# Pooling stage of a two-layer decoder trunk: the pool scale as one split row spread by TensorE, small loads moved, mixing reordered

## The chip, the cores and the metric

One core of a Trainium2 chip runs the whole program. The metric is the device time of one execution in microseconds. A core has five engines with queues of their own that run side by side and meet at semaphores: TensorE (PE; its weight loads are PEld), VectorE (DVE), ScalarE (ACT), GpSimd (POOL) and SyncE (SP). SP, ACT and POOL issue the DMAs. Each engine works its instructions strictly in the order in which the kernel issues them.

## The reference

A trunk of two layers over 512 tokens of width 1024, all float32. Layer 0 mixes tokens by causal pooling in four channel groups, layer 1 by differential attention; after each mixer and each FFN stands a LayerNorm over ALPHA times the input plus the branch. The change touches the pooling mixer alone:

```python
def _multiscale_pool(x, w, scale):
    xg = x.astype(jnp.float32).reshape(B, S, N_GROUPS, GROUP_W)
    cs = jnp.pad(jnp.cumsum(xg, axis=1), ((0, 0), (1, 0), (0, 0), (0, 0)))
    for g, win in enumerate(POOL_WINDOWS):          # 2, 4, 8, 16
        hi = cs[:, 1:, g]
        lo = jnp.pad(cs[:, :S + 1 - win, g], ((0, 0), (win - 1, 0), (0, 0)))
        cnt = jnp.minimum(t + 1, win).astype(jnp.float32)[None, :, None]
        pooled.append((hi - lo) / cnt)
    pooled = jnp.stack(pooled, axis=2)
    mixed = jnp.einsum('bsgc,gcd->bsgd', pooled - xg, w.astype(jnp.float32))
    return (mixed.reshape(B, S, D) * scale.astype(jnp.float32)).astype(x.dtype)

def reference(...):
    for i in range(DEPTH):
        ...
        x = _layernorm(ALPHA * x + h, ln_mix_g[i], ln_mix_b[i])
        x = _layernorm(ALPHA * x + _swiglu(x, w_gate[i], w_up[i], w_down[i]), ln_ffn_g[i], ln_ffn_b[i])
    return x
```

## The kernel before

Matrix products run in fp32r: each operand is split into a rounded high part and the rest, its low part, and three matmuls (high x high, high x low, low x high) make one product (`mm3`). The high part is a cast by ACT, the low part a subtraction by DVE (`split`; one time by POOL). After the pooling stage come the first FFN (`ffn(0, ...)`), the attention and the second FFN; their code is the same in both kernels. The first FFN's first matmuls read `xt`, the normed and transposed tokens 0 to 255, and the weight tiles w2 and w3; then w4 and w5 with the transposes of token blocks 2 and 3 between them.

The pooling stage works on four token blocks of 128 (`res[:, s]`, loaded by `load_x(s)`). Its steps, in the kernel's order:

- Loads. SP issues x block 0, x block 1, the first half of the pool scale (512 channels, broadcast over 128 partitions by the load itself), weight tile raw 0 (`fetch`), x block 2, the scale's second half, raw 1, x block 3, raw 2. ACT issues `d0`, the 16 x 16 corner with the counts of the first tokens. POOL issues four small loads: the rows of the LayerNorm gains and biases (`lrows`, two loads), the bias table (`tb`) and the one-hot lines (`oh_`).
- Constants. POOL makes `after`, a distance table, and `ident`. DVE makes `band` (L291) out of it: for each group a 128 x 144 matrix with 1/w where a token falls into the window, 128 columns for the block itself and 16 for the tail that reaches into the next block. `edge` is the same for block 0, with `d0` copied into its corner by ACT (L298). DVE subtracts the identity (L297), since the mixer takes pooled minus x.
- Warm-up. Seven matmuls on a zero tile (L303), in two records each.
- `shares(half, s, source, a, b, ...)` (L329): eight float32 matmuls, 16 records, that spread token block s over the accumulators `made[half, g]` of its half of the tokens: columns a to b of band or edge are the moving operand. The order on TensorE is: block 0 (144 columns), block 1 (128 columns), block 1's tail into the second half (16 columns), block 2 (144 columns), the mixing of the first half, block 3.
- `scale_weights(c)` (L306, L311): DVE multiplies the raw mixing weights by the scale. `pool_weights(c)` (L315) splits them into pw0 and pw1. `split_pooled` (L342) splits the accumulators into `ph` and `pl` (named pooled in the profile).
- `mixed(s, d)` (L353): 12 matmuls of 256 columns for half the output channels of token block s. Order before: (0,0), (1,0), (0,1), (1,1).
- `summed`, `spread_of`, `norm`: DVE adds the residual (L154), takes statistics (L161) and norms the block (L179); the power for it is on POOL (L170).
- Then the transposes of blocks 0 and 1 (L206), their evictions by ACT with gain and bias (L225) and the split into `xt`, the mixing of blocks 2 and 3, four matmuls for the bias lines (L406), and the FFN.

All eight PSUM banks hold `made` at first; the warm-up writes `made[1, 0]`, and a mixing accumulator takes the bank of a part of `made` that has been split. The order within each engine is the one in which the kernel is written (`manual_schedule`).

Of the kernel before, what the change touches and what calls it, by code (L numbers as in the profile page):

```python
# [11 lines left out]
F32 = mybir.dt.float32  # L12
# [5 lines left out]
P = 128  # L18
# [34 lines left out]
def trunk(ctx, tc, x, wall, pscale, lam_p, subln, table, lng, lnb, first, onehot, out):  # L53
# [27 lines left out]
    def load_x(s):  # L81
        nc.sync.dma_start(out=res[:, s, :], in_=x[s * P : (s + 1) * P, :])
# [8 lines left out]
    def fetch(upto):  # L91
        while fetched[0] < min(upto, total):
            c = fetched[0]
            raws[c] = keep.tile([P, 1024], F32, tag="raw", name=f"raw{c}", bufs=RAWS)
            nc.sync.dma_start(out=raws[c], in_=wall[c])
            fetched[0] += 1
# [146 lines left out]
    ctx.enter_context(tc.manual_schedule())  # L243
    with tc.tile_pool(name="pool", bufs=1) as pp:
        nc.scalar.preload_act_table_set("silu_and_others")
        load_x(0)
        d0 = pp.tile([16, 4, 16], F32, name="d0")
        nc.scalar.dma_start(out=d0, in_=first)
        load_x(1)
        scale = pp.tile([P, D], F32, name="scale")  # L250

        def load_scale(c):
            cc = slice(c * 512, (c + 1) * 512)
            nc.sync.dma_start(out=scale[:, cc], in_=pscale[:, cc].broadcast_to([P, 512]))

        load_scale(0)
        fetch(1)
        load_x(2)
        load_scale(1)
        fetch(2)  # L260
        load_x(3)
        fetch(3)

        still = pp.tile([P, P], F32, name="still")
        nc.vector.memset(still, 0.0)
        after = pp.tile([P, 144], F32, name="after")
        nc.gpsimd.iota(
            after, pattern=[[1, 144]], base=0, channel_multiplier=-1,
# [4 lines left out]
            base=0, channel_multiplier=-1,  # L273
        )
        make_identity(nc, ident)
        nc.gpsimd.memset(mhalf, -0.5)
        nc.gpsimd.memset(eps_t, EPS)
        tb = pp.tile([33, HEADS], F32, name="tb")
        nc.gpsimd.memset(tb, MASKED)
        lrows = pp.tile([2 * 2 * DEPTH * KB, P], F32, name="lrows")  # L280
        for i, t in enumerate((lng, lnb)):
            nc.gpsimd.dma_start(
                out=lrows[32 * i : 32 * (i + 1)], in_=t.rearrange("n (k p) -> (n k) p", p=P)
            )
        nc.gpsimd.dma_start(out=tb[:32, :], in_=table)
        oh_ = pp.tile([33, LINE], F32, name="oh_")
        nc.gpsimd.dma_start(out=oh_, in_=onehot)
        band = pp.tile([P, 4, 144], F32, name="band")
        edge = pp.tile([P, 4, 144], F32, name="edge")
        for g, w in enumerate(WINDOWS):  # L290
            nc.vector.tensor_scalar(  # L291
                band[:, g, :], after, scalar1=float(w), scalar2=1.0 / w, op0=ALU.is_lt, op1=ALU.mult
            )
        nc.scalar.copy(edge[:, :, P:], band[:, :, P:])
        own = ident.unsqueeze(1).to_broadcast([P, 4, P])
        for t in (edge, band):
            nc.vector.tensor_tensor(t[:, :, :P], band[:, :, :P], own, op=ALU.subtract)  # L297
        nc.scalar.copy(edge[:16, :, 0:16], d0)  # L298

        made = {(i, g): bank(f"pool{i}_{g}") for i in range(2) for g in range(4)}  # L300
        warm = made[1, 0]
        for i in range(WARM):
            nc.tensor.matmul(warm[:, 0:P], still, still, start=True, stop=True)  # L303
        pw = []

        def scale_weights(c, engine=nc.vector):  # L306
            raw = raws[c]
            for j in range(2):
                r = raw[:, j * 512 : (j + 1) * 512].rearrange("p (k e) -> p k e", k=2)
                e0 = c * 512 + j * GW  # L310
                engine.tensor_tensor(  # L311
                    r, r, scale[:, e0 : e0 + GW].unsqueeze(1).to_broadcast([P, 2, GW]), op=ALU.mult
                )

        def pool_weights(c, between=lambda: None):  # L315
            h, l = weight_pair(f"pw{c}") if c else first_pair
            raw = raws.pop(c)
            cols = [slice(j * 512, (j + 1) * 512) for j in range(2)]
            for cc in cols:
                nc.scalar.copy(h[:, cc], raw[:, cc])  # L320
            between()
            for cc in cols:
                nc.vector.tensor_tensor(l[:, cc], raw[:, cc], h[:, cc].bitcast(F32), op=ALU.subtract)
            pw.append((h, l))
            divided[0] += 1
# [3 lines left out]
        def shares(half, s, source, a, b, o, first=False):  # L329
            for k in range(KB):  # L330
                g = k // 2
                c = (k % 2) * 256 + o
                mm(
                    made[half, g][:, c : c + b - a],
                    res[:, s, k * P : (k + 1) * P],
                    source[:, g, a:b],
                    start=first and k % 2 == 0,
                    stop=False,
                    skip_group_check=True,
                )  # L340

        def split_pooled(half, *groups):  # L342
            for g in groups:
                c = slice(half * 256, (half + 1) * 256)
                split(
                    ph[:, 2 * g : 2 * g + 2, c],
                    pl[:, 2 * g : 2 * g + 2, c],
                    made[half, g].rearrange("p (k t) -> p k t", k=2),
                )
# [3 lines left out]
        def mixed(s, *ds):  # L353
            if s not in mixes:
                mixes[s] = [bank(f"mix{s}_{d}") for d in range(2)]
            acc = mixes[s]
            for g in [2 * d + i for d in ds for i in range(2)]:
                h, l = pw[g // 2]
                o = acc[g // 2][:, (g % 2) * GW : (g % 2 + 1) * GW]
                for k in range(2):  # L360
                    kk = 2 * g + k
                    c0 = (g % 2) * 512 + k * GW
                    mm3(
                        o,
                        (ph[:, kk, s * P : (s + 1) * P], pl[:, kk, s * P : (s + 1) * P]),
                        (h[:, c0 : c0 + GW], l[:, c0 : c0 + GW]),
                        k == 0,
                        k == 1,
                    )

        def summed(s, *ds):
            for d in ds:
                residual(s, d, mixes[s][d])
                stat(0, s, d)

        shares(0, 0, edge, 0, 144, 0, True)
        shares(0, 1, band, 0, P, P)
        shares(1, 1, band, P, 144, 0, True)
        scale_weights(0)
        pool_weights(0)  # L380
        split_pooled(0, 0, 1)
        shares(1, 2, band, 0, 144, 0)
        mixed(0, 0)
        scale_weights(1)
        split_pooled(0, 2, 3)
        pool_weights(1)
        mixed(1, 0)
        mixed(0, 1)
        fetch(3 + RAWS)
        tbh = pp.tile([33, HEADS], F32R, name="tbh")  # L390
# [2 lines left out]
        split(tbh, tbl, tb)  # L393
        nc.scalar.copy(ohr, oh_)

        ready(3, nc.gpsimd)
        mixed(1, 1)
        shares(1, 3, band, 0, P, P)
        summed(0, 0, 1)
        spread_of(0, 0)  # L400
        def lines_sum():
            b = [bank(f"line{i}") for i in range(2)]
            for i in range(2):
# [3 lines left out]
                mm(bb, tbl, ohr[:, cc], start=False, stop=True)  # L407
            return b

        summed(1, 0)  # L410
        norm(0, 0)
        summed(1, 1)
# [969 lines left out]
```

## Time and profile before

| what | value |
|---|---|
| three runs | 942.6, 942.99, 941.13 us; median 942.6 |
| profiled execution: its own time | 944.93 us |
| its span, first to last instruction | 943.1 us |
| mean granted TensorE clock | 0.993 |
| HBM read, written | 159.64 MB, 36.72 MB |

The span is what the profile shows of the profiled execution; 1.8 us of its time lie outside the span. Every time below counts from the start of the span. In the timeline a row is: start, duration, engine, line, operation, output<-inputs, shapes, count of instructions merged, and in brackets the idle time of the engine before it with what ended it. In a table of windows a row is the stretch, its length, then for PE, PEld, DVE, ACT and POOL the busy time with the number of instructions in brackets, then the granted TensorE clock, the share of the DMA engines and GB/s. A row of the waits gives engine and line, what it waited for, the sum, how often, the longest. A row of the grouped instructions gives the count, then busy time and mean ns, then idle time before. A row of the DMA issues gives tile, queue, count, size and the median time from issue to landing. PE's matmuls overlap, so the step from one start to the next is the price of one in a row, and its own duration is longer.

### The profile page before, as it was taken

What the parts mean: (1) busy time and instruction counts of PE and PEld (TensorE: products, weight loads), DVE (VectorE), ACT (ScalarE), POOL (GpSimd) and SP (SyncE); (2) the same over time, 40 slices, a digit from 0 to 9 for tenths busy, and PEclk for the clock granted to TensorE, in tenths of its full rate; (3) what the DMA queues carried; (4) which work ended last, traced back from release to release, by engine and by line L of the source; (5) the groups of instructions that cost most, each with busy time, mean ns of one, the idle gap of its engine ahead of it and who ended that gap; (6) DMA issues with size and microseconds to landing.
All of it is one profiled execution on the core that took longest, in us unless ns stands there. A gap on an engine that the chain in (4) does not pass through costs nothing. (4 is left out here: it accounts for less than half of the span.)

```text
span 943.1 us, 15993 instructions
## 1 busy us (share of the span) xinstructions
PE 929.6 (99%) x6255; PEld 855.5 (91%) x6255; DVE 817.1 (87%) x1208; ACT 500.8 (53%) x802; POOL 104.6 (11%) x134
## 2 busy tenths in 40 slices
PE   9999999999999999999999999999999999999996
PEld 8999999999988888988888888999999999988884
DVE  6999999999988898688777676799999999988798
ACT  4744545554653557655566553834545554653460
POOL 2121121110001101000000000211111110001101
PEclk9999999999999999999999999999999999999998
DMA  8388998985878964332222122389988886878962
GB/s 295 96 241 268 290 282 256 267 281 192 259 242 283 347 218 141 135 92 95 79 80 87 59 90 90 112 263 273 280 263 262 253 280 204 249 241 280 336 223 89
DMA packets 73643, 197.40 MB, mean 209 GB/s; under 512 B 6562, under 2 KB 17986, under 8 KB 73568
## 3 DMA queue, kind: packets, MB, share of 16 engines
q1 hardware_dynamic: 33984, 114.44, 36.7%
q0 software_dynamic: 15952, 47.31, 19.2%
q10 hardware_dynamic: 23632, 34.63, 10.0%
q8 instruction: 49, 0.80, 0.3%
q14 instruction: 26, 0.21, 0.1%
HBM read 159.64 MB, written 36.72 MB: 208 GB/s over the span
## 5 line engine op out<-in xcount | busy, mean ns | idle before, releaser
L565 DVE TENSOR_TENSOR raw<-raw,raw 128x1024 f32<-128x1024 f32 x72 | 87.8, 1219 | 0.6
L105 ACT CAST xs<-hid 128x512 fp32r<-128x512 f32 (+1 forms) x60 | 34.7, 581 | 28.5 <-DVE hid L730 28.5
L106 DVE TENSOR_TENSOR xs<-hid,xs 128x512 fp32r<-128x512 f32 (+1 forms) x60 | 38.4, 642 | 7.8 <-ACT xs L105 7.8
L225 ACT ACTIVATE y<-pt,gbT 128x128 f32<-128x128 f32 x92 | 34.6, 456 | 18.9 <-PE pt L206 18.7
L1104 ACT ACTIVATE p<-p,mn 128x128 f32<-128x128 f32 (+3 forms) x64 | 35.4, 554 | 14.9 <-DVE mn L1099 14.9
L661 POOL DMA_DIRECT2D b<-in_wall x24 | 18.0, 795 | 159.2 <-DMA tsum<-b 88.0
L722 POOL DMA_DIRECT2D xs<-ssum x24 | 17.4, 727 | 142.2 <-PE Q L877 119.7
L837 ACT ACTIVATE sg<-sg 128x512 f32<-128x512 f32 x18 | 11.4, 633 | 33.6 <-DVE sg L828 33.6
L170 POOL TENSOR_TENSOR rs<-rs,mhalf 128x1 f32<-128x1 f32 x16 | 11.7, 734 | 151.9 <-DVE rs L169 151.9
L1099 DVE CUSTOM_DVE_ANT_0 p<-s,bias 128x128 f32<-128x128 f32 (+3 forms) x64 | 28.1, 485 | 0.0
L106 POOL TENSOR_TENSOR sql<-sq,sqh 128x512 fp32r<-128x512 f32 x7 | 9.0, 1293 | 165.3 <-ACT sqh L105 165.3
L106 DVE TENSOR_TENSOR xt<-y,xt 128x512 fp32r<-128x512 f32 x23 | 15.5, 687 | 12.4 <-ACT xt L105 12.4
L698 ACT CAST v<-u 128x512 fp32r<-128x512 f32 x22 | 13.7, 621 | 22.2 <-DVE u L696 22.1
L661 POOL DMA_DIRECT2D hid<-in_wall x20 | 14.7, 736 | 94.8 <-DMA tsum<-hid 37.9
L820 ACT COPY hid<-C 128x512 f32<-128x512 f32 x18 | 10.6, 588 | 24.1 <-PE C L809 24.0
L161 DVE BATCH_NORM_STATS2 st<-res 128x6 f32<-128x512 f32 x32 | 22.2, 695 | 1.1
L106 DVE TENSOR_TENSOR heads<-k,heads 128x512 fp32r<-128x512 f32 x8 | 5.5, 692 | 20.2 <-ACT heads L105 20.2
L824 DVE TENSOR_TENSOR hid<-C,hid 128x512 f32<-128x512 f32 x18 | 12.4, 691 | 10.8 <-PE C L809 9.2
L662 POOL DMA_DIRECT2D b<-in_wall x12 | 14.8, 1229 | 56.2 <-DMA b<-in_wall 50.5
L105 ACT CAST heads<-k 128x512 fp32r<-128x512 f32 x8 | 4.7, 588 | 26.3 <-PE k L125 26.3
L1118 DVE SCALAR_TENSOR_TENSOR p<-p,sm,p 128x128 f32<-128x128 f32 (+3 forms) x32 | 17.7, 552 | 1.1
L1094 PE MATMUL s<-heads 64*128 64x256 f32 (+2 forms) x192 | 17.9, 330 | 0.0
(1132 smaller groups left out, 3769.0 us busy)
## 6 DMA issues: line engine op xcount, KB each, us to landing
raw<-in_wall SPq DMA_DIRECT2D x122, 512.0 KB, 4.5
r<-tsum SPq DMA_DIRECT2D x40, 512.0 KB, 4.5
b<-in_wall POOLq DMA_DIRECT2D x36, 512.0 KB, 6.1
hid<-in_wall POOLq DMA_DIRECT2D x30, 512.0 KB, 5.9
r<-in_wall SPq DMA_DIRECT2D x30, 512.0 KB, 4.8
tsum<-b ACTq DMA_DIRECT2D x24, 512.0 KB, 5.2
ssum<-v ACTq DMA_DIRECT2D x22, 512.0 KB, 4.0
tsum<-hid ACTq DMA_DIRECT2D x20, 512.0 KB, 5.4
```

The costliest lines, as they stand in the source:

```text
L105: nc.scalar.copy(dst_h, src)
L106: (low or nc.vector).tensor_tensor(dst_l, src, dst_h.bitcast(F32), op=ALU.subtract)
L161: nc.vector.bn_stats(stats[n, s][:, d, :], res[:, s, d * 512 : (d + 1) * 512])
L225: nc.scalar.activation(y[:, k, :], src, AF.Identity, bias=b, scale=g)
L565: tt(t, raws[pair[0]], raws[pair[1]], op=ALU.add)
L661: nc.gpsimd.dma_start(out=t[:, j], in_=src[:, j])
L662: nc.gpsimd.dma_start(out=t[:, 0], in_=src[:, :, 1], accum_op=ALU.add)
L722: nc.gpsimd.dma_start(out=t.bitcast(F32), in_=ssum[:, 0 if p == "P7" else 1, :, r, :])
L1094: nc.tensor.matmul(accs[c][:, :wide], a[r, qs], b[r, :wide], start=i == 0, stop=i == 2)
L1099: nc.vector.tensor_tensor_reduce(out=p, in0=accs[c][:, :w], in1=biases[h][:, w - 1 :: -1] if w < S else biases[h][:, ::-1], op0=ALU.add, o ...
L1104: nc.scalar.activation(p, p, AF.Exp, bias=mn[:, q, c : c + 1], scale=-1.0, accum_out=sm[:, q, c : c + 1],)
L1118: nc.vector.scalar_tensor_tensor(p0[:, r], p0[:, r], sm[:, q, 0:1], p1[:, r], op0=ALU.mult, op1=ALU.add)
```

## The change

The pool scale is no longer broadcast by the load. One row of 1024 numbers (`scrow`) comes in on ACT's queue. ACT and DVE split it into a high row at partition 0 and a low row at partition 32 of a zeroed tile `srows`; `pick` is a stationary tile with ones in rows 0 and 32 and zeros elsewhere, so that two matmuls of 512 columns (`spread`) put the scale on all 128 partitions, into the banks of `made[1, 1]` and `made[1, 2]`. DVE's scaling reads the first half straight from PSUM; ACT copies the second half to SBUF.

`d0` is loaded by SP behind x block 0; the four small loads go to SP behind x block 3 and ahead of raw 2. `band` becomes 256 columns wide, with POOL's memset filling columns 144 on with zeros, and the tail of block 1 is multiplied with 128 columns instead of 16, now after the pool weights' first split in the program's order. `scale_weights(1)` moves ahead of the split of the first half. The mixing order becomes (0,0), (0,1), (1,0), (1,1). `lines_sum` is only moved in the text.

```diff
@@ -243,26 +243,23 @@
     ctx.enter_context(tc.manual_schedule())
     with tc.tile_pool(name="pool", bufs=1) as pp:
         nc.scalar.preload_act_table_set("silu_and_others")
+        scrow = pp.tile([1, D], F32, name="scrow")
+        nc.scalar.dma_start(out=scrow, in_=pscale)
         load_x(0)
         d0 = pp.tile([16, 4, 16], F32, name="d0")
-        nc.scalar.dma_start(out=d0, in_=first)
+        nc.sync.dma_start(out=d0, in_=first)
         load_x(1)
-        scale = pp.tile([P, D], F32, name="scale")
-
-        def load_scale(c):
-            cc = slice(c * 512, (c + 1) * 512)
-            nc.sync.dma_start(out=scale[:, cc], in_=pscale[:, cc].broadcast_to([P, 512]))
-
-        load_scale(0)
         fetch(1)
         load_x(2)
-        load_scale(1)
         fetch(2)
         load_x(3)
-        fetch(3)
 
         still = pp.tile([P, P], F32, name="still")
         nc.vector.memset(still, 0.0)
+        pick = pp.tile([P, P], F32R, name="pick")
+        nc.vector.memset(pick.bitcast(F32), 0.0)
+        for r in (0, 32):
+            nc.vector.memset(pick[r : r + 1].bitcast(F32), 1.0)
         after = pp.tile([P, 144], F32, name="after")
         nc.gpsimd.iota(
             after, pattern=[[1, 144]], base=0, channel_multiplier=-1,
@@ -273,43 +270,65 @@
             base=0, channel_multiplier=-1,
         )
         make_identity(nc, ident)
+        srows = pp.tile([P, D], F32R, name="srows")
+        for c in range(2):
+            nc.gpsimd.memset(srows[:, c * 512 : (c + 1) * 512].bitcast(F32), 0.0)
+        band = pp.tile([P, 4, 2 * P], F32, name="band")
+        nc.gpsimd.memset(band[:, :, 144:], 0.0)
         nc.gpsimd.memset(mhalf, -0.5)
         nc.gpsimd.memset(eps_t, EPS)
         tb = pp.tile([33, HEADS], F32, name="tb")
         nc.gpsimd.memset(tb, MASKED)
         lrows = pp.tile([2 * 2 * DEPTH * KB, P], F32, name="lrows")
         for i, t in enumerate((lng, lnb)):
-            nc.gpsimd.dma_start(
+            nc.sync.dma_start(
                 out=lrows[32 * i : 32 * (i + 1)], in_=t.rearrange("n (k p) -> (n k) p", p=P)
             )
-        nc.gpsimd.dma_start(out=tb[:32, :], in_=table)
+        nc.sync.dma_start(out=tb[:32, :], in_=table)
         oh_ = pp.tile([33, LINE], F32, name="oh_")
-        nc.gpsimd.dma_start(out=oh_, in_=onehot)
-        band = pp.tile([P, 4, 144], F32, name="band")
+        nc.sync.dma_start(out=oh_, in_=onehot)
+        fetch(3)
         edge = pp.tile([P, 4, 144], F32, name="edge")
         for g, w in enumerate(WINDOWS):
             nc.vector.tensor_scalar(
-                band[:, g, :], after, scalar1=float(w), scalar2=1.0 / w, op0=ALU.is_lt, op1=ALU.mult
+                band[:, g, 0:144], after, scalar1=float(w), scalar2=1.0 / w, op0=ALU.is_lt, op1=ALU.mult
             )
-        nc.scalar.copy(edge[:, :, P:], band[:, :, P:])
+        nc.scalar.copy(edge[:, :, P:], band[:, :, P:144])
         own = ident.unsqueeze(1).to_broadcast([P, 4, P])
-        for t in (edge, band):
-            nc.vector.tensor_tensor(t[:, :, :P], band[:, :, :P], own, op=ALU.subtract)
+
+        def split_scale(c):
+            cc = slice(c * 512, (c + 1) * 512)
+            nc.scalar.copy(srows[0:1, cc], scrow[:, cc])
+            nc.vector.tensor_tensor(
+                srows[32:33, cc], scrow[:, cc], srows[0:1, cc].bitcast(F32), op=ALU.subtract
+            )
+
+        nc.vector.tensor_tensor(edge[:, :, :P], band[:, :, :P], own, op=ALU.subtract)
         nc.scalar.copy(edge[:16, :, 0:16], d0)
+        split_scale(0)
+        nc.vector.tensor_tensor(band[:, :, :P], band[:, :, :P], own, op=ALU.subtract)
+        split_scale(1)
 
         made = {(i, g): bank(f"pool{i}_{g}") for i in range(2) for g in range(4)}
         warm = made[1, 0]
         for i in range(WARM):
             nc.tensor.matmul(warm[:, 0:P], still, still, start=True, stop=True)
         pw = []
-
-        def scale_weights(c, engine=nc.vector):
+        scale = pp.tile([P, 512], F32, name="scale")
+        spreads = [made[1, 1], made[1, 2]]
+
+        def spread(c):
+            nc.tensor.matmul(
+                spreads[c], pick, srows[:, c * 512 : (c + 1) * 512], start=True, stop=True
+            )
+
+        def scale_weights(c):
             raw = raws[c]
             for j in range(2):
                 r = raw[:, j * 512 : (j + 1) * 512].rearrange("p (k e) -> p k e", k=2)
-                e0 = c * 512 + j * GW
-                engine.tensor_tensor(
-                    r, r, scale[:, e0 : e0 + GW].unsqueeze(1).to_broadcast([P, 2, GW]), op=ALU.mult
+                by = (scale if c else spreads[0])[:, j * GW : (j + 1) * GW]
+                nc.vector.tensor_tensor(
+                    r, r, by.unsqueeze(1).to_broadcast([P, 2, GW]), op=ALU.mult
                 )
 
         def pool_weights(c, between=lambda: None):
@@ -374,17 +393,19 @@
                 stat(0, s, d)
 
         shares(0, 0, edge, 0, 144, 0, True)
+        spread(0)
+        spread(1)
         shares(0, 1, band, 0, P, P)
-        shares(1, 1, band, P, 144, 0, True)
         scale_weights(0)
+        nc.scalar.copy(scale, spreads[1])
         pool_weights(0)
+        shares(1, 1, band, P, 2 * P, 0, True)
+        scale_weights(1)
         split_pooled(0, 0, 1)
         shares(1, 2, band, 0, 144, 0)
+        pool_weights(1)
+        split_pooled(0, 2, 3)
         mixed(0, 0)
-        scale_weights(1)
-        split_pooled(0, 2, 3)
-        pool_weights(1)
-        mixed(1, 0)
         mixed(0, 1)
         fetch(3 + RAWS)
         tbh = pp.tile([33, HEADS], F32R, name="tbh")
@@ -393,11 +414,6 @@
         split(tbh, tbl, tb)
         nc.scalar.copy(ohr, oh_)
 
-        ready(3, nc.gpsimd)
-        mixed(1, 1)
-        shares(1, 3, band, 0, P, P)
-        summed(0, 0, 1)
-        spread_of(0, 0)
         def lines_sum():
             b = [bank(f"line{i}") for i in range(2)]
             for i in range(2):
@@ -407,6 +423,12 @@
                 mm(bb, tbl, ohr[:, cc], start=False, stop=True)
             return b
 
+        ready(3, nc.gpsimd)
+        mixed(1, 0)
+        mixed(1, 1)
+        shares(1, 3, band, 0, P, P)
+        summed(0, 0, 1)
+        spread_of(0, 0)
         summed(1, 0)
         norm(0, 0)
         summed(1, 1)
```

## The prediction

> **What bounds the kernel now.** I read the page first, then the waits of TensorE over the whole span, then the start: windows of the clock, the timeline engine by engine, the landings of the loads.
>
> ```profile
> PE 929.6 (99%) x6255; PEld 855.5 (91%) x6255; DVE 817.1 (87%) x1208; ACT 500.8 (53%) x802; POOL 104.6 (11%) x134
> ...
> PE pt L206 <- DVE res L179: 1.5, 3, 0.6
> PE pool L303 <- DVE still L265: 1.1, 1, 1.1
> PE mix L125 <- DVE pooled L106: 1.0, 1, 1.0
> PE pool L333 <- DMA res<-in_x: 0.4, 1, 0.4
> ```
>
> TensorE is the bound, and nearly all of its few waits lie in the pooling stage at the start, which the change rewrites. So the end moves with the moment at which the first FFN matmuls start, unless a new wait appears behind it. Two more losses at the start are no waits:
>
> ```profile
> 12.00:16.00 4.00, 4.00 (x22) 4.00 (x21) 4.00 (x8) 3.39 (x8) 0.00 (x0) 0.57 1.03 410
> 24.00:26.00 2.00, 1.04 (x8) 0.84 (x7) 1.93 (x6) 1.97 (x6) 0.55 (x1) 0.93 0.00 0
> 26.00:30.00 4.00, 4.00 (x24) 4.00 (x24) 4.00 (x6) 3.97 (x11) 0.00 (x0) 0.61 0.00 2
> ```
>
> The granted clock (the number behind the POOL column) means half speed for 2 x 0.43 x 4 = 3.4 us between 12 and 16, and for 0.3 + 3.1 = 3.4 us between 24 and 30: each time 1.7 us of work is lost. Ahead of the second TensorE is busy for only 1.04 of 2 us. Ahead of the first stands this:
>
> ```profile
> 3.96 0.24 ACT L298 COPY edge<-d 16x64 f32<-16x64 f32 x1 [1.41 <-DMA d<-in_first]
> ...
> 4.38 0.33 SPq L82 DMA_DIRECT2D res<-in_x  x1
> ...
> 4.50 2.56 PE L333 MATMUL pool<-edge,res 128*128 128x144 f32 x16
> ...
> 6.90 3.64 PE L333 MATMUL pool<-band,res 128*128 128x128 f32 x32
> ...
> 10.94 3.15 PE L333 MATMUL pool<-band,res 128*128 128x144 f32 x16 [0.40 <-DMA res<-in_x]
> ...
> L333 PE MATMUL pool<-band,res 128*128 128x128 f32 x16 | 1.9, 275 | 0.0
> L333 PE MATMUL pool<-band,res 128*128 128x16 f32 x16 | 1.9, 258 | 0.0
> ```
>
> The 32 records from 6.90 are 16 of 128 columns (token block 1) and 16 of 16 columns (its tail). Both kinds take some 1.8 us of it: in the tail the array has an eighth of the work in the same time. Then 0.4 us pass until x block 2 lands. That is the low stretch ahead of the half clock.
>
> **Loads.** x block 0 lands at about 4.4: TensorE starts at 4.50 though ACT's copy was done at 4.20, and SP's last x load leaves at 4.38 when a semaphore of a landed one comes free.
>
> ```profile
> 0.74 0.86 SPq L82 DMA_DIRECT2D res<-in_x  x2
> ...
> res<-in_x SPq DMA_DIRECT2D x2, 512.0 KB, 4.4
> ...
> 5.00:6.75 1.75, 1.75 (x15) 1.75 (x14) 0.00 (x0) 0.00 (x0) 0.00 (x0) 1.00 0.52 150
> 7.00:9.00 2.00, 2.00 (x21) 2.00 (x19) 0.00 (x0) 0.00 (x0) 0.00 (x0) 1.00 1.05 420
> ...
> 9.12 1.29 DVE L311 TENSOR_TENSOR raw<-raw,scale 128x512 f32<-128x512 f32 x2 [5.32 <-DMA raw<-in_wall]
> ```
>
> x block 1 goes out at about 1.2 and lands at 5.6; TensorE has block 2 at 10.94 (above). Gone are the two 256 KB broadcasts of the scale; the first holds the queues from 5 to 6.75 at 150 GB/s, where 420 follow. Without it raw 0 comes right behind x block 1: 512 KB at 420 GB/s are 1.25 us, so I estimate 6.9 for raw 0 (9.1 now) and 8.2 for x block 2. Neither is then waited for. The four small rows leave POOL's queue and follow x block 3 on SP; raw 2 stands behind them, 3.5 us ahead of its reader at about 15, which covers the 0.4 us of each issue; without this cover, 1.7 us. POOL is idle there, so its four issues less save nothing.
>
> **Start.** d0 moves from ACT's queue to SP's, behind x block 0. Its landing is bounded by x block 0 (4.4) and x block 1 (5.6); I take 4.5, since its 16 short rows stand between two blocks. ACT's copy (0.24) ends near 4.8 and TensorE starts at 4.9, 0.4 later. Behind that copy ACT now has the scale's two row copies, and behind each of these DVE has a difference, with the band's subtraction between the two. I price one row by its length, as 128 rows (from below, nothing):
>
> ```profile
> 3.11 0.69 DVE L297 TENSOR_TENSOR band<-band,ident 128x512 f32<-128x512 f32 x1
> ...
> 9.85 1.22 ACT L320 CAST pw0h<-raw 128x512 fp32r<-128x512 f32 x2 [5.64 <-DVE raw L311]
> ...
> 33.56 0.39 PE L406 MATMUL line<-ohr,tbh 33*8 33x512 f32 x1
> 33.79 0.39 PE L407 MATMUL line<-ohr,tbl 33*8 33x512 f32 x1
> ```
>
> ACT 4.8 to 5.4 and to 6.0; DVE 5.5 to 6.2, band to 6.8, second difference to 7.4. The first 144-column group ends at 4.9 + 2.4 = 7.3, so the two spreads follow without a real wait. One costs between the 0.23 from one 512-column row to the next and the 0.39 of the row; I take the step, since they issue back to back: 7.3 to 7.8. POOL's three memsets, 1472 columns, take 2.3 us at the rate of ident's (128 in 0.20) or 3.5 at that of its slow subtraction (1024 in 2.43), and are done at 4.3 to 5.5; the first srows half, a third of it, is due at 4.8. DVE's memsets of pick fit before POOL hands over at 1.5.
>
> ```profile
> 1.43 0.20 POOL masks.py:197 MEMSET ident<- 128x128 f32 x1
> ...
> 1.51 0.76 DVE L291 TENSOR_SCALAR band<-after 128x144 f32<-128x144 f32 x4 [0.51 <-POOL after L271]
> ...
> 16.61 2.43 POOL L106 TENSOR_TENSOR w2l<-raw,w2h 128x1024 fp32r<-128x1024 f32 x1 [12.25 <-ACT w2h L105]
> ```
>
> **First half.** DVE scales from 7.8 on (spread 0 is out), not from 9.12. The same six pairs follow, 7.5 us to the first sum, and 0.2 more for ACT, whose copy of the second spread (0.6) stands ahead of pw0h: 15.4, not 16.6. TensorE: block 1 and its tail, 1.8 each (the tail issues as fast at 128 columns as at 16, so the widening is free), to 11.4; block 2 by its columns 2.0, to 13.4, when pooled is just ready (7.8 + 0.2 + 3.9 + the pair that now comes first, 1.2 = 13.1). The tail's group 1 reuses the bank of spread 0 and so waits for the scaling, done at 9.1 against 10.0. Then four mixings and block 3:
>
> ```profile
> 16.59 0.67 DVE L154 SCALAR_TENSOR_TENSOR res<-res,mix 128x512 f32<-128x512 f32 x1
> ...
> 17.47 0.28 PE L123 MATMUL mix<-pw1h,pooled 128*128 128x256 f32 x1
> ...
> 20.35 1.95 PE L333 MATMUL pool<-band,res 128*128 128x128 f32 x16
> ...
> 19.11 0.69 DVE L154 SCALAR_TENSOR_TENSOR res<-res,mix 128x512 f32<-128x512 f32 x1 [1.12 <-PE mix L125]
> ```
>
> 24 matmuls from 17.47 to 20.35 make 1.44 for a mixing. 13.4 + 5.8 + 1.8 = 21.0, where now 20.35 + 1.8 = 22.15: 1.2 earlier for TensorE and for ACT's casts behind it. In the new order the second sum of block 0 has its matmuls one mixing sooner; DVE's wait of 1.12 at 19.11 goes, and DVE is 2.3 ahead at the splits of the second half.
>
> **Second half.**
>
> ```profile
> 23.87 1.51 ACT L225 ACTIVATE y<-pt,gbT 128x128 f32<-128x128 f32 x4
> ...
> 24.67 1.28 DVE L106 TENSOR_TENSOR pooled<-pool,pooled 128x512 fp32r<-128x512 f32 x2
> ...
> 31.49 0.68 DVE L106 TENSOR_TENSOR xt<-y,xt 128x512 fp32r<-128x512 f32 x1
> ...
> 41.70 0.81 DVE L179 TENSOR_SCALAR res<-res,mv,rs 128x1024 f32<-128x1024 f32 x1 [0.73 <-POOL rs L170]
> ...
> 42.43 1.22 DVE L106 TENSOR_TENSOR w5l<-raw,w5h 128x1024 fp32r<-128x1024 f32 x1
> ...
> 43.83 1.03 PE L206 MATMUL pt<-ident,res 128*128 128x128 f32 x8
> ...
> 44.94 0.28 PE L125 MATMUL u<-xt,w5l 128*128 128x256 f32 x1
> ```
>
> TensorE gets pooled's first low part at 25.4 - 2.3 = 23.1; 1.2 of mixing, 1.0 of transposes, three mixings (4.3) and 0.8 of lines make it ready for the FFN at 30.4, if the clock stays full. ACT's row of evictions from 23.87 is dense and only 1.2 earlier, and DVE's low halves wait for it: xt comes at 32.2 - 1.2 = 31.0. The FFN, now from 34.2, could start 3.2 earlier. But DVE's norm of block 3 ends at 42.5 and is read at 43.8; w5l ends at 43.65, read at 44.94. Each has 1.3 of slack and is 1.2 earlier. TensorE waits there for the difference. **The sum: 2.5 us.** With the second half clock TensorE is ready at 32.1, 2.1 earlier: nearly the same. The profiled execution's span goes from 943.1 to 940.6, its time from 944.9 to 942.4; it ran 2.3 above the runs' median, which goes from 942.6 to 940.1.
>
> **Rivals.**
>
> *The first half clock stays.* Block 2 and mixing 0 lose 1.7: block 3 ends at 22.7, 0.55 later than now, ACT with it; of 1.3 of slack 0.75 is left: 941.8. For it: the second half clock followed a stall of some 1 us, which no wider tail touches. Against it: the narrow records are the only low stretch before the first. [...]
>
> *d0 late.* Landing with x block 1, at 5.6, it moves everything by 1.1: 941.2. From 5.1 on the gain is under 0.2%. For it: the 512 KB on each side of it in one queue.
>
> *Slower: the band's builders queue behind the memset of its tail.* POOL fills columns 144 on before DVE writes the others. If a tile's writers are kept in order, DVE starts band at 4.3 to 5.5 instead of 1.51 and TensorE at 6.2 to 7.4, 1.3 to 2.5 behind my 4.9, with one half clock (1.7) after the longer idling: 21.0 becomes 22.3 to 25.2, and with 1.3 of slack against 22.15 the time is 941.4 to 944.3, slower once POOL's memsets end past about 5. I price it at 944.3. Against it:
>
> ```profile
> 2.31 0.24 ACT L294 COPY edge<-band 128x64 f32<-128x64 f32 x1 [0.28 <-DVE band L291]
> 2.39 0.69 DVE L297 TENSOR_TENSOR edge<-band,ident 128x512 f32<-128x512 f32 x1
> ```
>
> ACT and DVE write two parts of edge at the same time.
>
> *More.* DVE's slack proves larger and the FFN keeps its 3.2: 939.4.
>
> **How the numbers follow.** Forecast 0.55, first half clock 0.16, late d0 0.13, slower 0.08, more 0.08. The time is the forecast's. The range, 939.0 to 942.2, takes in the gain of 3.2 and both middle rivals, with the spreads at their upper price (0.3 more); the slower case is left out. 0.2%, 1.9 us, is about what a measurement of this kernel can tell from no change. Faster by more: the 0.08, nearly all of the forecast, a little of the late d0: 0.62. Slower by more: 0.09. Within it: 0.29.
>
> **What would show it.** Right: TensorE's first pooling matmul near 4.9, DVE's scaling near 7.8, no wait for x block 2, full clock from 8 to 20, block 3 issued by 21, no DVE wait for mixing, the FFN from about 31, and a new TensorE wait of some 0.5 us near 41 for norm or w5l. Wrong: DVE's band after 4; a granted clock of 0.5 between 12 and 16; an FFN less than 1 us earlier; or one 2 to 3 us earlier with the end unmoved.

## The result and the profile after

The changed kernel takes 945.44 us (median of 12 runs, 943.13 to 946.51), the kernel before 942.5 us in runs on the same chip (12 runs, 941.13 to 943.62). The ratio is 1.0033, 95% interval 1.0024 to 1.0042: slower, by 2.9 us, where 2.5 us faster was predicted. The profiled execution of the changed kernel took 946.51 us with a span of 944.7 us.

The busy times and the waits of TensorE over the whole span, changed kernel:

```profile
PE 929.6 (98%) x6257; PEld 855.6 (91%) x6257; DVE 821.3 (87%) x1213; ACT 501.7 (53%) x805; POOL 103.9 (11%) x133
...
PE pt L206 <- DVE res L179: 2.1, 2, 1.5
PE pool L315 <- DVE still L258: 1.1, 1, 1.1
PE mix L125 <- DVE pooled L106: 1.0, 1, 1.0
PE pool L352 <- ACT edge L307: 0.6, 1, 0.6
PE q L124 <- DVE xt L106: 0.2, 1, 0.2
```

TensorE's busy time is what it was (929.6). The 0.4 us wait for x block 2 is gone; in its place stand 0.6 us for ACT's corner copy, and the wait for DVE's norm grew from 1.5 to 2.1 us, 1.5 of it at one place. DVE's busy time grew by 4.2 us; the profile has only 5 more instructions of it (1213 for 1208). One instruction that stood there before holds half of that growth. The timeline of DVE and POOL around it, changed kernel:

```profile
9.51 1.28 DVE L330 TENSOR_TENSOR raw<-raw,pool 128x512 f32<-128x512 f32 x2 [1.85 <-PE pool L321]
...
15.70 1.28 DVE L106 TENSOR_TENSOR pooled<-pool,pooled 128x512 fp32r<-128x512 f32 x2
...
16.75 2.43 POOL L106 TENSOR_TENSOR w2l<-raw,w2h 128x1024 fp32r<-128x1024 f32 x1 [13.03 <-ACT w2h L105]
...
16.90 2.30 DVE L106 TENSOR_TENSOR tbl<-tb,tbh 33x8 fp32r<-33x8 f32 x1
...
19.13 0.67 DVE L154 SCALAR_TENSOR_TENSOR res<-res,mix 128x512 f32<-128x512 f32 x1
```

The same instruction in the kernel before:

```profile
16.51 0.15 DVE L106 TENSOR_TENSOR tbl<-tb,tbh 33x8 fp32r<-33x8 f32 x1
```

`tbl` is the low half of the bias table, eight numbers on 33 partitions. It took 0.15 us before and 2.30 us now. Before, it was issued at 16.51 and POOL's subtraction of w2's low half followed at 16.61, a lead of 0.10 us. Now POOL issues at 16.75 and DVE at 16.90; DVE's instruction ends at 19.20, with POOL's (19.18), and the first residual sum stands right behind it. POOL's instruction takes 2.43 us both times. So the two profiles have 0.15 us where DVE came first and 2.30 us where POOL did. What held DVE's instruction no trace shows. The expectations below call the account in which the order of issue decides the port theory, though no trace shows a port.

The second loss lies at the start. Windows of the changed kernel, four of them cut in steps of 3.41 us from the trace's clock records at 9.10 and 26.17:

```profile
2.28:5.69 3.41, 2.77 (x13) 2.48 (x13) 1.29 (x4) 1.19 (x4) 1.44 (x6) 1.00 0.89 341
5.69:9.10 3.41, 3.41 (x16) 3.41 (x16) 1.91 (x3) 0.34 (x1) 0.00 (x0) 1.00 0.98 369
9.10:12.50 3.40, 3.40 (x30) 3.31 (x30) 2.90 (x5) 2.67 (x5) 0.00 (x0) 1.00 1.04 358
12.00:16.00 4.00, 4.00 (x36) 4.00 (x35) 4.00 (x8) 3.60 (x8) 0.00 (x0) 1.00 1.03 400
...
22.76:26.17 3.41, 1.53 (x12) 1.21 (x11) 3.27 (x8) 2.16 (x6) 0.22 (x2) 1.00 0.00 0
...
26.00:30.00 4.00, 3.27 (x17) 3.27 (x18) 4.00 (x8) 3.94 (x10) 0.55 (x1) 0.57 0.00 0
```

And the timeline of the start, changed kernel:

```profile
1.05 3.35 PE L315 MATMUL pool<-still 128*128 128x128 f32 x14 [1.05 <-DVE still L258]
...
1.63 1.11 DVE L293 TENSOR_SCALAR band<-after 128x144 f32<-128x144 f32 x4
...
4.75 0.24 ACT L307 COPY edge<-d 16x64 f32<-16x64 f32 x1 [1.74 <-DMA d<-in_first]
...
5.04 4.20 PE L352 MATMUL pool<-edge,res 128*128 128x144 f32 x16 [0.64 <-ACT edge L307]
...
8.88 0.83 PE L321 MATMUL pool<-srows,pick 128*128 128x512 f32 x2
```

From 5.69 to 9.10 TensorE is busy all the time but gets through 16 records, and through 30 in the next window: half speed, although the column of the granted clock says 1.00 (the first clock record of this trace, at 9.10, is where full speed begins). So block 0's group takes 3.84 us (5.04 to 8.88) and not 2.4, the spreads come at 8.88, and DVE's scaling starts at 9.51. The clock between 12 and 16 is full now. The half clock behind the second half's stall (26.17 to 29.58) is still there; in the 3.41 us ahead of it TensorE is busy for 1.53.

The end of the stage, changed kernel:

```profile
20.83 1.95 PE L352 MATMUL pool<-band,res 128*128 128x128 f32 x16
...
24.47 1.06 PE L206 MATMUL pt<-ident,res 128*128 128x128 f32 x8 [1.49 <-DVE res L179]
...
26.00 1.28 DVE L106 TENSOR_TENSOR pooled<-pool,pooled 128x512 fp32r<-128x512 f32 x2
26.73 0.58 PE L125 MATMUL mix<-pw0h,pooled 128*128 128x256 f32 x1 [0.96 <-DVE pooled L106]
...
35.26 0.39 PE L123 MATMUL g<-xt,w2h 128*128 128x256 f32 x1
```

And the kernel before:

```profile
34.23 0.39 PE L123 MATMUL g<-xt,w2h 128*128 128x256 f32 x1
```

TensorE has block 3 only 0.5 us later than before (20.83 against 20.35), but then waits 1.49 us for the norm and 0.96 us for pooled, since DVE is 1.3 us late (26.00 against 24.67). The FFN starts 1.03 us later. Of the 1.6 us between the two spans the other 0.6 lie behind the last matmul.

### The profile page after: what moved, and what is told of

Read it like the earlier page. It is cut to its first block, busy times and chain, and to the rows that moved or that the text cites. A ratio compares the mean times of both kernels' runs of the same rounds, so it can differ in the third digit from the quotient of the medians.

```text
span 944.7 us, 16005 instructions
## 1 busy us (share of the span) xinstructions
PE 929.6 (98%) x6257; PEld 855.6 (91%) x6257; DVE 821.3 (87%) x1213; ACT 501.7 (53%) x805; POOL 103.9 (11%) x133
```

## The experiments

Each median stands beside the median of the kernel before in the same set of runs; "against before" is the difference of the two.

**e1, e2, e3: the two suspects, one at a time and together**

e1 gives the bias table's subtraction to POOL, where it stands in one queue with w2's:

```diff
-        split(tbh, tbl, tb)
+        split(tbh, tbl, tb, low=nc.gpsimd)
```

> Changed kernel, but the small 33 x 8 subtraction tbl goes from DVE to POOL. Port theory: in the changed kernel this subtraction took 2.30 us instead of 0.15, because POOL's w2l subtraction (2.43 us, both inputs in SBUF) began 0.15 us ahead of it; without it DVE's first sum begins near 17.0 instead of 19.1, the FFN 1.5 to 2.2 us earlier, and the time falls from 945.4 to 943.2 to 943.9. Rival, cold start alone: TensorE's late first half, not DVE, sets the second half, and the time stays within 0.5 of 945.4.

e2 puts `d0` back on ACT's queue, ahead of the scale's row:

```diff
-        scrow = pp.tile([1, D], F32, name="scrow")
-        nc.scalar.dma_start(out=scrow, in_=pscale)
         load_x(0)
         d0 = pp.tile([16, 4, 16], F32, name="d0")
-        nc.sync.dma_start(out=d0, in_=first)
+        nc.scalar.dma_start(out=d0, in_=first)
+        scrow = pp.tile([1, D], F32, name="scrow")
+        nc.scalar.dma_start(out=scrow, in_=pscale)
```

> Changed kernel with d0 again on ACT's queue, ahead of the scale's row. Cold-start theory: TensorE starts at 4.5 instead of 5.04, so the warm-up flows into the pooling and the clock is granted at the first chance; DVE scales near 8.0 instead of 9.5, all moves by 1.0 to 1.5, the time is 944.0 to 944.5; the 2.3 us subtraction stays. Rival: only the 0.5 of the late start is won, 944.9. Port theory alone: no more than 0.3, since DVE is still blocked after POOL's start.

e3 has both edits:

> Both edits together. If the two losses are separate, the gains add: 941.8 to 942.8, no slower than the kernel before. If one hides the other, the time is that of the better one, near 943.5.

| kernel | median (range), us | ratio, 95% interval | against before | scaling | first sum | FFN starts |
|---|---|---|---|---|---|---|
| changed | 945.44 (943.13 to 946.51) | 1.0033 (1.0024 to 1.0042) | +2.9 | 9.51 | 19.13 | 35.26 |
| e1, tbl on POOL | 943.44 (942.32 to 945.22) | 1.0015 (1.0006 to 1.0024) | +1.3 | 8.85 | 16.24 | 31.25 |
| e2, d0 on ACT | 943.46 (942.70 to 945.79) | 1.0017 (1.0007 to 1.0026) | +1.3 | 7.43 | 17.37 | 33.58 |
| e3, both | 941.89 (941.64 to 943.34) | 1.0000 (0.9991 to 1.0008) | -0.25 | 7.61 | 15.03 | 30.04 |

The three columns on the right are from one profiled execution of each: the slowest of its 12 runs for the changed kernel, the fastest of theirs for e1 and e3. So the differences of these columns are larger than those of the medians. The two edits add up: each takes off about 1.6 us, with the other (e1 to e3, e2 to e3) and without it. The mean granted clock of each timed run adds to this: it is 0.995 or less in 11 of 12 runs of the changed kernel, in 5 of 12 of e2 and in none of e1 and e3. (One half clock of 3.4 us lowers it by 0.0018.) So a half clock goes with the collision of the two subtractions; in the profiles of the changed kernel and of e2 it is the one behind the second half's stall. The one run of the changed kernel at a higher mean, 0.997, took 943.13 us. Of what d0 is worth in e2, a part can be that the half clock comes less often there; how much is open. The timeline of e1, DVE and POOL:

```profile
14.52 0.66 POOL L106 TENSOR_TENSOR tbl<-tb,tbh 33x8 fp32r<-33x8 f32 x1 [10.79 <-ACT tbh L105]
...
16.14 2.43 POOL L106 TENSOR_TENSOR w2l<-raw,w2h 128x1024 fp32r<-128x1024 f32 x1 [0.95 <-ACT w2h L105]
16.24 0.68 DVE L154 SCALAR_TENSOR_TENSOR res<-res,mix 128x512 f32<-128x512 f32 x1
...
16.95 0.69 DVE L161 BATCH_NORM_STATS2 st<-res 128x6 f32<-128x512 f32 x1
```

DVE's first sum, with one input in PSUM, runs beside the same POOL instruction at its usual 0.68 us, and so do the statistics. Only the subtraction with both inputs in SBUF was held. In e2, where the table stays on DVE, it still takes 2.30 us.

**e4: the same collision made in the kernel before**

```diff
+        ready(3, nc.gpsimd)
         split(tbh, tbl, tb)
         nc.scalar.copy(ohr, oh_)
-        ready(3, nc.gpsimd)
```

> Kernel before, with the 33 x 8 subtraction issued behind the split of w2, so that it meets POOL's subtraction. Port theory: it takes 2.0 to 2.4 us instead of 0.15, DVE's first sum starts near 18.9 instead of 16.6, of which 1.1 are hidden by DVE's wait for the mixing at 19.11, and the time rises by about 1.0, to 943.5. Rival (the long duration has another cause, such as the operand's late arrival): 0.15 us as before and 942.5.

The edit lets POOL's subtraction go out ahead of DVE's. Timeline of e4:

```profile
16.43 2.43 POOL L106 TENSOR_TENSOR w2l<-raw,w2h 128x1024 fp32r<-128x1024 f32 x1 [12.09 <-ACT w2h L105]
16.47 2.40 DVE L106 TENSOR_TENSOR tbl<-tb,tbh 33x8 fp32r<-33x8 f32 x1
...
18.80 0.67 DVE L154 SCALAR_TENSOR_TENSOR res<-res,mix 128x512 f32<-128x512 f32 x1
```

A POOL lead of 0.04 us is enough: 2.40 us in place of 0.15. Median 944.02 us (943.36 to 946.92), ratio 1.0021 (1.0012 to 1.0030), 1.9 us above before. Nothing else of the change is in this kernel. The edit moves ACT's cast of w2 as well, but `tbl` does not start later for it (16.47, before 16.51); so the order of these two subtractions has this price by itself. It is more than the 1.0 expected. Half clocks come with it: the mean granted clock is 0.995 or less in 9 of 12 runs of e4, and in 4 of the 35 runs of the kernel before beside it.

**e7: the gap ahead of block 0 filled**

```diff
-WARM = 7
+WARM = 8
```

on top of e1, so d0 still comes by SP's queue.

> Changed kernel with tbl on POOL and d0 still on SP's queue behind x block 0, but eight warm-up matmuls instead of seven, which fill the idle time before the pooling (the warm-up then ends near 4.9, the pooling starts near 5.0 to 5.2 as it does). Clock theory: what the late d0 costs is the gap, which delays the full clock; with it filled the median falls from 943.4 to 942.0 to 942.6. Rival: it costs by the later start itself, and the median stays at 943.2 to 943.6.

Median 942.59 us (942.07 to 943.73), ratio 1.0003 (0.9994 to 1.0012), +0.1 against before; e1 has +1.3, with intervals that overlap. The wait of TensorE for ACT's corner copy, e7:

```profile
PE pool L352 <- ACT edge L307: 0.2, 1, 0.2
```

The first pooling matmul comes no earlier (5.01; changed kernel 5.04), and in e3 it comes only 0.2 us earlier (4.84). So much of what d0's late landing costs seems not to be the later start but the gap in TensorE's work that it leaves. The 3.41 us ahead of full speed, e3 and then e7:

```profile
2.06:5.47 3.41, 2.99 (x15) 2.72 (x14) 1.67 (x5) 1.43 (x4) 1.67 (x6) 1.00 0.83 336
```

```profile
3.33:6.74 3.41, 3.25 (x15) 2.95 (x14) 1.41 (x3) 1.28 (x3) 0.40 (x4) 1.00 0.86 273
```

After windows with 2.99 and 3.25 us of work full speed was given; after the changed kernel's window with 2.77, which held the whole gap of 0.64 us, it was not, and came one window later. Where the windows fall differs from execution to execution: e1's begin elsewhere, its gap of 0.74 us is cut in two, and it had full speed from 4.73. That the clock goes by windows of 3.41 us is an estimate from the clock records of two profiles. In the changed kernel they stand at 9.10, 26.17 and 29.58 us: 17.07 us are five times 3.413, and the half clock takes 3.41. In the kernel before the half clocks go from 12.08 to 15.49 and from 25.73 to 29.15, and the 10.24 us between them are three times 3.413. That the busy time of a window decides is not shown: no run here sets it by itself. If it does, the limit lies, again as an estimate, between the changed kernel's 2.77 us and e3's 2.99; both are from single executions.

**e5, e6, e9: the width of the tail, and the kernel before once more**

e5 is the kernel before with the wide tail alone, e6 is e3 with the narrow tail:

```diff
-        shares(1, 1, band, P, 144, 0, True)
+        shares(1, 1, band, P, 2 * P, 0, True)
```

(e5, with the wider band and its memset; e6 has the reverse.)

> Kernel before with the wider tail alone (band 256 columns wide, zeros from 144 on, 128 columns for the tail of block 1). Narrow-tail theory: the half clock of 3.4 us that some runs have near 12 us goes away; the runs near 942.6 and 944 move to 941.3 and the median falls from 942.1 to about 941.4. Rival (only a long idle stretch lowers the clock, so that the tail's width does not matter): 942.1, with the same share of runs at 942.6.

> The kernel with both repairs (tbl on POOL, d0 on ACT's queue), its tail narrow again (16 columns). Narrow-tail theory: the half clock comes back between 8 and 16 us in part of the runs, the median rises from 941.9 by 0.5 to 1.5. Rival: the width is worth nothing, 941.9 within 0.4.

> The kernel before, unchanged, for a second profile. Theory of the unlucky base: the profile that the prediction summed over had two half-clock windows, and most runs have none or one; this one shows none or one, the FFN's start between 31.5 and 33.0 instead of 34.2, and a span of 939.5 to 941.5. Rival (the two windows belong to the kernel): two windows near 12 and 26, the FFN from 34.2, a span near 943.

e5: 941.87 us (941.26 to 943.31), ratio 0.9995 (0.9986 to 1.0003). e6: 941.77 us (941.62 to 943.29), ratio 0.9998 (0.9989 to 1.0007). Neither shows a worth of the width. Neither profile has a half clock. e9, the kernel before in another profiled execution, took 942.99 us. Its windows:

```profile
12.00:16.00 4.00, 4.00 (x25) 4.00 (x24) 4.00 (x8) 3.39 (x7) 0.00 (x0) 0.69 1.03 411
...
26.00:30.00 4.00, 4.00 (x35) 3.86 (x34) 4.00 (x7) 3.97 (x10) 0.00 (x0) 1.00 0.01 2
```

The second half clock, of which the prediction's profile had 3.1 us between 26 and 30, is not there, and the FFN starts at 32.93 instead of 34.23. The first one is. So the half clocks come and go between executions of the same kernel, and the prediction's profile had both. Of 35 timed runs of it, taken beside e1 to e4, 17 lie between 941.1 and 941.8 us, 18 between 942.1 and 944.6; the profiled execution, at 944.93, lies above all of them. The 18 fastest have a mean granted clock of 0.997 or 0.998, the other 17 one of 0.996 or less; the profile had 0.993.

The prediction's slack at block 3 was that execution's too. The norm of block 3 and the transposes that read it, e9 and then e5:

```profile
41.84 0.81 DVE L179 TENSOR_SCALAR res<-res,mv,rs 128x1024 f32<-128x1024 f32 x1 [0.73 <-POOL rs L170]
...
42.80 1.07 PE L206 MATMUL pt<-ident,res 128*128 128x128 f32 x8
```

```profile
40.62 0.81 DVE L179 TENSOR_SCALAR res<-res,mv,rs 128x1024 f32<-128x1024 f32 x1 [0.73 <-POOL rs L170]
...
41.57 1.07 PE L206 MATMUL pt<-ident,res 128*128 128x128 f32 x8
```

From the norm's end to the transposes 0.15 us pass in e9 and 0.14 in e5. In the prediction's profile it was 1.3 (42.51 to 43.83): there the second half clock had made the FFN 1.3 us later than in e9, and DVE's norm no later (41.70 against 41.84).

**e10, e11: the other parts of the change taken back from e3**

e10 has the old order of mixing:

```diff
         mixed(0, 0)
+        mixed(1, 0)
         mixed(0, 1)
...
         ready(3, nc.gpsimd)
-        mixed(1, 0)
         mixed(1, 1)
```

> The kernel with both repairs, mixing again in the old order (0,0), (1,0), (0,1), (1,1). Theory that DVE's and ACT's evictions set the second half: DVE waits about 1 us again for the second sum and is later at the splits, but ACT's evictions hide it; the time stays within 0.4 of 941.9. Rival, as the prediction had it: the wait is passed on, and the time rises by 0.8 to 1.1.

Median 942.30 us (941.95 to 944.11), ratio 1.0005 (0.9995 to 1.0014). DVE's wait for the second sum is back, as its timeline shows:

```profile
18.24 0.69 DVE L154 SCALAR_TENSOR_TENSOR res<-res,mix 128x512 f32<-128x512 f32 x1 [1.29 <-PE mix L125]
```

In e3 the second sum starts at 16.35 without a wait. The median differs by 0.4 us, with intervals that overlap: what the order is worth in time stays open.

e11 has the scale by two broadcast loads again, without the row, `pick` and the spreads:

```diff
-        scrow = pp.tile([1, D], F32, name="scrow")
-        nc.scalar.dma_start(out=scrow, in_=pscale)
         load_x(1)
+        load_scale(0)
         fetch(1)
         load_x(2)
+        load_scale(1)
         fetch(2)
...
-        spread(0)
-        spread(1)
-        nc.scalar.copy(scale, spreads[1])
```

> The kernel with both repairs, but the scale loaded by two broadcasts again (no row, no spreads; mixing order, wide tail and small loads as changed). DVE then scales near 9 instead of 7.5 and the FFN starts 1.0 to 1.5 later. Theory that DVE's norms behind the FFN's start cap the lead: the time rises by no more than 0.5, to at most 942.4. Rival: the full lead of the row counts, 942.9 to 943.4.

Median 943.84 us (943.75 to 945.02), ratio 1.0023 (1.0013 to 1.0033), +1.7 against before and 1.95 above e3. In the profile DVE scales at 8.73 (e3: 7.61), the first sum stands at 16.79 (15.03), and TensorE has a new wait:

```profile
PE mix L123 <- DVE pooled L106: 1.5, 1, 1.5
```

The expectation that DVE's cap further back would swallow the lost start was wrong; the rival, under which it shows in full, came closer. So the split row is worth about 2 us within this order of the program. e11 keeps the new order, in which the first mixing needs more of DVE's work done; that fits its being slower than the kernel before, which has the same large loads, but was not tried by itself.

**e8, e12: DVE relieved behind the start**

Both are e3 with one more low half on POOL: w4's (e8), or w3's, whose whole split also moves behind the turned halves of blocks 0 and 1 (e12).

```diff
-        ready(4)
         y = turned_half(0, 1, 1, pts[1][1], second)
         split_turned(1, 0, turned_half(0, 1, 0, pts[1][0]))
         split_turned(1, 1, y)
+        ready(4, nc.gpsimd)
```

(e12; e8 has `ready(5, nc.gpsimd)` ahead of `summed(2, 0, 1)` in place of `ready(5)`.)

> The kernel with both repairs, and the low half of w4 subtracted by POOL, ahead of the sums of blocks 2 and 3, not by DVE. DVE-slack theory: behind the FFN's start TensorE waits for the norm of block 3 and loses 0.7 of its lead there; DVE is 1.2 earlier then, and the median falls from 941.9 by 0.5 to 0.8, to 941.1 to 941.4. Rival: POOL's subtraction blocks DVE's two-input subtractions or norms, and the time stays or rises.

> The kernel with both repairs, and the split of w3 behind the evictions of blocks 0 and 1, its low half on POOL. DVE and ACT are 1.0 to 1.2 earlier at xt and at the norms of blocks 2 and 3. DVE-cap theory: TensorE keeps its lead of 4.2 behind the FFN's start, of which it lost 1.4 there, and the median falls from 941.9 by 0.7 to 1.3, to 940.6 to 941.2. Rival: the lead is lost at another place, and the time stays at 941.6 to 941.9.

e8: 941.62 us (940.96 to 942.87), ratio 0.9994 (0.9984 to 1.0003), no difference that can be told. e12: 940.46 us (940.31 to 941.16), ratio 0.9984 (0.9975 to 0.9993): faster than the kernel before by 1.7 us. The timeline of e3 from the start of the FFN to the transposes of blocks 2 and 3:

```profile
30.04 0.38 PE L123 MATMUL g<-xt,w2h 128*128 128x256 f32 x1
...
30.60 0.38 PE L124 MATMUL g<-xt,w2h 128*128 128x256 f32 x1 [0.17 <-DVE xt L106]
...
36.60 1.06 PE L206 MATMUL pt<-ident,res 128*128 128x128 f32 x8
...
40.07 0.81 DVE L179 TENSOR_SCALAR res<-res,mv,rs 128x1024 f32<-128x1024 f32 x1 [0.73 <-POOL rs L170]
...
41.03 1.06 PE L206 MATMUL pt<-ident,res 128*128 128x128 f32 x8 [0.49 <-DVE res L179]
```

The same in e12:

```profile
30.20 2.44 POOL L106 TENSOR_TENSOR w3l<-raw,w3h 128x1024 fp32r<-128x1024 f32 x1 [7.50 <-ACT w3h L105]
...
35.96 1.04 PE L206 MATMUL pt<-ident,res 128*128 128x128 f32 x8
...
38.65 0.82 DVE L179 TENSOR_SCALAR res<-res,mv,rs 128x1024 f32<-128x1024 f32 x1 [0.73 <-POOL rs L170]
...
39.71 1.04 PE L206 MATMUL pt<-ident,res 128*128 128x128 f32 x8
```

The FFN starts no earlier in e12 (30.11), but without DVE's 1.2 us for w3 the norm of block 3 is 1.4 us earlier, TensorE no longer waits for it, and 1.4 us are gained at the end. In e3, DVE behind the start was the limit, and at more than one place. From the FFN's start to block 2's transposes e3 takes 6.56 us and e12 5.85, so 0.7 us are lost there, with a wait for DVE's xt at 30.60; from block 2's transposes to block 3's it is 4.43 against 3.75, another 0.7. e8 fits this: with w4 off DVE the second stretch takes 3.78 us (37.10 to 40.88), without a wait for the norm, while the first still takes 6.55, from 30.55.

## Why the prediction was wrong

Against the median of before it said -2.5 us and +2.9 were measured. The 5.4 us between them are 1.6 for the table's subtraction, 1.6 for d0 and, as what is left, 2.2 for the base. Three steps failed.

**"The same six pairs follow, 7.5 us to the first sum": failed by an instruction that had no term.** The step counted the pairs and nothing between them and the sum. The pairs were right (7.4 us from scaling to first sum in e1 and e3); the changed kernel took 9.6, and 2.15 of that is tbl. The quoted row of POOL's subtraction at 16.61 stood in the prediction as a rate for memsets; that a DVE instruction with both inputs in SBUF starts only 0.10 us ahead of it had no term. Rows of the kernel before had its place, the starts at 16.51 and 16.61, and POOL's 2.43 us; that DVE is held nearly as long once POOL goes first, none of them showed. The changed kernel (2.30 us) and e4 (2.40 us) do. The collision takes away DVE's lead, hence the waits of 1.49 and 0.96 us and the half clock behind them. e2, with the collision, has waits of the same size (1.5 and 1.0) and a half clock too; e1 and e3, without it, wait 0.5 at most at any of these places and have no half clock.

**"d0 4.5, TensorE starts at 4.9, 0.4 later; the first group ends at 7.3": the start was right, what follows was not.** The corner copy came at 4.75 and the first matmul at 5.04. It was priced as a shift of 0.4; the group's duration was carried over from a profile in which TensorE's warm-up ran into it with a gap of 0.1 us. In the profiled execution, with 0.64 us of idling, the full clock came later and the group took 3.84 us; e1's execution, with 0.74, had it in time, from 4.73. That it depends on where the windows fall fits both, but no run tried it by itself. The spreads, put at 7.3 to 7.8, came at 8.88. The rival "d0 late" had the right culprit, but its landing with x block 1 at 5.6 did not happen.

**"Each has 1.3 of slack" and "it ran 2.3 above the runs' median", taken as constants: failed.** The sum was made against an execution with two half-clock windows, and 2.3 us were then taken off both sides. But most runs of before lack at least one of those windows: e9, with one, took 942.99 us, and 17 of 35 timed runs lie at 941.1 to 941.8, 3.2 to 3.8 below the profiled one, about the price of two. What the typical run had not lost was counted as gain. The slack of 1.3 us at block 3's norm was part of it: e9 and e5 have 0.15, so there TensorE already runs at DVE's pace, and an earlier FFN wins only what DVE wins. e3's norm of block 3 is 0.55 us ahead of e5's (40.07 against 40.62), and its transposes 0.54. e3, with both faults mended, beats that execution by 3.3 us (941.64 against 944.93), more than the 2.5 forecast, and the median of before by 0.25 us only, within its interval of 0.9991 to 1.0008.

**"Widening removes the first half clock": not settled.** It is gone in the changed kernel (1.00 from 12 to 16), and e5 has none either, but nor has e6 with 16 columns, where x block 2 isn't waited for and the window's cut falls elsewhere. A mean granted clock of 0.996 or less stands in 16 of 33 runs of before beside e5, in 3 of 11 of e5, in 1 of 12 of e3 and in 1 of 10 of e6. So beside the new loads and order no worth of the width is seen, and in the kernel before 11 runs are too few to tell. The long idle stretch that e5's rival asks for is not there ahead of the first half clock of the kernel before: TensorE is busy for 3.02 of the 3.41 us up to it. That the tail issues as fast at 128 columns was right: 48 records without a break in 5.69 us in e3 and 5.70 in e6.

**The mixing order: right as a mechanism** (no wait for mixing on DVE in the changed kernel, 1.29 us again in e10), unmeasured as time.

**The cap at block 3: right as a limit by DVE, but not the only place.** TensorE waits 0.49 us for the norm at 41.03 in e3, where "some 0.5 near 41" was written, and e12 shows that DVE held the gain. But half of the 1.4 us were lost ahead of block 2's transposes, a part of it in the wait for xt, for which the prediction let the FFN start at 31.0 and not at 30.04; between that start and block 3 it had no loss. e5 agrees that the lead is lost: with its FFN from 31.72 its span is 939.8, and e3's, from 30.04, is 939.9.

**The small rows on SP and the rest:** x block 2 and raw 0 are not waited for, as said. The rival in which the band's builders queue behind the memset of the tail had the right sign by another mechanism: DVE began band at 1.63.

## What to carry to other kernels

When an edit changes the order of two engines by some tenths of a microsecond, list the DVE instructions with two inputs in SBUF that stand beside a POOL instruction of the same kind, and see which is issued first: a 33 x 8 subtraction of 0.15 us lost a lead of 0.10 us and took 2.30 us beside a neighbour of 2.43, while DVE's sum with one input in PSUM kept its 0.68 us beside the same neighbour in e1. Before a sum is made against one profiled execution, compare its time and its granted clock with those of the timed runs; what sets it apart from them, here two half clocks, is no gain to be had, and a slack read from it can be theirs. A gap of 0.64 us in TensorE's work ahead of its first long run seems to have cost more than its length here (the group behind it took 3.84 us and not 2.4), so fill such a gap or close it.

## What the runs showed of the hardware

**A small subtraction nearly as long as its neighbour.** The 33 x 8 subtraction took 2.30 us (changed kernel) and 2.40 us (e4) behind a POOL instruction of 2.43 us that went ahead of it by 0.15 and 0.04 us, and 0.15 us with a lead of 0.10 (kernel before). POOL's time did not change. No other size was met in this place.

**Half speed that the granted clock doesn't show.** Ahead of the changed kernel's first clock record, at 9.10, the column says 1.00 while TensorE runs at half its speed (16 records in 3.41 us, then 30 in 3.40). Block 0's 16 records take 3.84 us there and 1.94 in e2 (4.51 to 6.45).

**Ahead of a half clock.** The 3.41 us right ahead of a half clock, up to its clock record, for TensorE alone (busy time with instructions, granted clock, DMA share, GB/s); the kernel before, two windows:

```profile
8.67:12.08 3.41, 3.02 (x27) 1.00 1.04 365
22.32:25.73 3.41, 1.81 (x13) 1.00 0.00 0
```

A window of e11, with columns alike, that no half clock followed:

```profile
11.70:15.11 3.41, 1.86 (x16) 1.00 1.05 327
```

1.81 us of work in the window, 1.53 in the changed kernel and 1.36 in e2 led to a half clock; 1.86 in e11 and 2.32 in e5 (20.18 to 23.60) did not. But 3.02 did as well where the window held narrow matmuls of 16 columns. So busy time alone is not what counts; that the narrow ones count for less fits, but no run here tried it by itself. All of these are single executions.
